# A feed forward in three token blocks in place of four, with seven-product multiplication in both of its weight matrices throughout

## The chip, the core and the metric

The kernel runs on one core of a Trainium2 chip, in one launch. The core has five engines that the text speaks of: PE (TensorE, the matrix multiplier), DVE (VectorE), ACT (ScalarE), POOL (GpSimd) and SP, whose queue issues every DMA of this kernel. The metric is device time in microseconds (us), the median of several runs. A difference of about 0.5% (12 us) is what a measurement of this kernel can tell from none.

## The reference, cut to what matters

One layer of a hybrid encoder: a mixer (a gated spatial MLP beside gated DeltaNet heads), then a feed forward. There are 2048 prompt tokens and 32 sample tokens, 2080 in all; the model is 1024 wide, the feed forward 4096. Everything is float32. The change touches the feed forward and the norm behind it alone:

```python
h = rmsnorm(x, norm_ffn_g[l]) * (1 + sc2) + sh2
x = x + gt2 * (jnp.square(jax.nn.relu(h @ w_up[l])) @ w_down[l])
...
y = rmsnorm(x, final_norm_g)
```

`h @ w_up` is (2080 x 1024) by (1024 x 4096), and `@ w_down` is (2080 x 4096) by (4096 x 1024).

## The kernel before

**How a float32 product is made.** A float32 value is split into a high part in PE's rounded type (`fp32r`) and the rest. `split` does it in two instructions: ACT copies the value into the high part, and DVE (or POOL) subtracts it from the value. A product then takes three matmuls (`mm3`): high weight by high value, high weight by low value, low weight by high value.

**Seven products instead of eight.** A 2 x 2 block product normally takes eight block products. The kernel uses a scheme of the Strassen-Winograd kind with seven, in which sums and differences of the quarters of both operands are multiplied. In the up multiplication the weights' sums S1 to S4 (`s1` to `s4` in `up_weights`) are made by POOL in block 0, split, and stored in DRAM (`su_d`); later blocks read them back. In the down multiplication, seven-product where `plain` is false, the weights' sums lie in `sd_d` as plain float32, and the values' differences T1 to T4 are made by POOL (`hidden`).

**Tiling.** The 2080 tokens are cut into `NB` = 4 blocks of two groups (g = 0, 1) of `G` = 260 tokens, so a matmul has 260 columns. The hidden width of 4096 is cut into 16 steps s of 256. An up step (`ffn_up`) has seven products of four k tiles, each an `mm3`: 84 matmuls. Two up steps (s = 2q, 2q + 1) make the hidden values of one q. A down q (`ffn_down`) has two steps u; each takes four quarters of the weights, makes seven products of four `mm3`, 84 matmuls, and adds the results to the accumulators `acc` in SBUF by DVE (`add`). Where `plain` holds, in block 0 and in q = 7 of every block, `ffn_down8` makes eight products, 96 matmuls a step.

**Order of the work.** In `feed_forward`, a block begins with two up steps; then down steps and up steps of the next q take turns. Around them: `h2_values(b)` normalises a block's input, builds its seven sums and stores them in DRAM (`th_d`), after up step 8 of the block before; `h2_load(b)` loads and splits them into `hp` (28 pieces in `BH` and `BL`), after up step 15 of the block before; `settle` adds the residual ahead of q = 6; `square` and `final` make the last norm and the output.

**Scheduling.** Every call records an instruction with its operands; `schedule` then lays out all of them by a list scheduler with a cost for each, due times taken from the matmuls, and a rule that a DVE and a POOL instruction with SBUF inputs alone take turns. The order on each engine's queue is fixed by that before the launch. Buffers are rings: `uw` (eight places of split up weights), `dw` (six of down weights), `uraw` and `draw` (raw weights), `rp8`, `rpa`, `rpb` (split hidden values), "fe" (six pieces for h2), "fk" (the first inner half's values, `keep`). A ring's place is written again only when its readers are done. PSUM's eight banks go round by `take` and `give`.

Of the kernel before, what the change touches and what calls it, by code (L numbers as in the profile page):

```python
# [31 lines left out]
G = 260  # L32
NB = T // (2 * G)
# [5 lines left out]
NSLOT = 25  # L39
# [283 lines left out]
class Kern:  # L323
# [211 lines left out]
    def setup(self):  # L535
# [103 lines left out]
        self.sd_d = [[dt(f"sd_d{u}_{i}", [P, 512]) for i in range(4)] for u in range(16)]  # L639
# [744 lines left out]
    def ffn_places(self):  # L1384
        rg = self.ring
        e = [(s, G * e) for s in (6, 7, 16, 22, 23) for e in range(4)]
        for tag, n in (("fe", 6), ("fs", 2), ("fx", 1), ("fp", 1), ("fu", 2), ("fv", 1), ("fr", 3), ("fk", 4)):
            rg(tag, e[:n], (P, G))
            e = e[n:]

    def fsegs(self, b, g):
        return [(0, G - NS, 0), (G - NS, NS, 1)] if (b, g) == (NB - 1, 1) else [(0, G, 0)]

    def h2_values(self, b):

        t0 = 2 * G * b
        r = [self.new("fs") for _ in range(2)]
        for g in range(2):
            self.dma(r[g], self.r2_d[:, t0 + G * g : t0 + G * g + G])
        for k in range(4):  # L1400
            h = []
            for kk in (k, k + 4):
                for g in range(2):
                    x = self.new("fe")
                    self.dma(x, self.x2_d[kk][:, t0 + G * g : t0 + G * g + G])
# [6 lines left out]
            put = lambda i, x: self.dma(self.th_d[b % 2][i][:, k], x)  # L1412
            put(0, b11)
            t1 = self.new("fe")
# [6 lines left out]
            t2 = self.new("fe")  # L1421
# [5 lines left out]
    def h2_load(self, b):  # L1427
        for i in range(7):
            for k in range(4):
                x = self.new("fe")  # L1430
                self.dma(x, self.th_d[b % 2][i][:, k])
                self.split(*self.hp[i][k], x, POOL if b and k % 2 else DVE)
# [11 lines left out]
    def operand(self, ring, x):  # L1444
        hi, lo = self.turn(ring)
        self.split(hi, lo, x)
        return hi, lo

    def up_weights(self, b, s):

        quad = lambda q: self.i["w_u"][s, q]
        if b == 0:
            a11, a12, a21, a22 = (self.raw(self.uraw, quad(q)) for q in range(4))
            s1, s2 = (self.turn(self.uraw) for _ in range(2))
            self.tt(s1, a21, a22, ALU.add, POOL)
            self.tt(s2, s1, a11, ALU.subtract, POOL)
        out = []

        def sum_(i, x):
            if b == 0:  # L1460
                hl = self.operand(self.uw, x)
                for e in range(2):
                    self.dma(self.su_d[s][i][e], hl[e].f32())
            else:
                hl = self.turn(self.uw)
                for e in range(2):
                    self.act(hl[e], self.raw(self.uraw, self.su_d[s][i][e]), AF.Copy)
            out.append(hl)

        plain = lambda q, x: out.append(self.operand(self.uw, x if b == 0 else self.raw(self.uraw, quad(q))))  # L1470
        if b:
            s1 = s2 = s3 = s4 = a11 = a12 = a22 = None
        plain(0, a11)
        sum_(1, s2)
        sum_(0, s1)
        if b == 0:
            s3 = self.turn(self.uraw) if len(self.uraw) > 6 else a11
            self.tt(s3, a11, a21, ALU.subtract, POOL)
        sum_(2, s3)
        if b == 0:  # L1480
            s4 = s2
            self.tt(s4, a12, s2, ALU.subtract, POOL)
        sum_(3, s4)
        plain(1, a12)
        plain(3, a22)
        return out

    def down_weights(self, b, u):

        quad = lambda q: self.i["w_d"][u, q]  # L1490
        if self.plain(b, u // 2):
            a = [self.raw(self.draw, quad(q)) for q in range(4)]
            out = [self.operand(self.dw, x) for x in a]
            if b == 0 and u % 2 == 0 and u < 14:
                a11, a12, a21, a22 = a
                for i, (o, x, y, op) in enumerate(((a22, a21, a22, ALU.add), (a21, a11, a21, ALU.subtract),
                                                   (a11, a22, a11, ALU.subtract), (a12, a12, a11, ALU.subtract))):
                    self.tt(o, x, y, op, POOL)
                    self.dma(self.sd_d[u][(0, 2, 1, 3)[i]], o)
            return out  # L1500
        return self.down_sums(b, u)

    def down_sums(self, b, u):
        quad = lambda q: self.i["w_d"][u, q]
        get = lambda x: self.raw(self.draw, x)
        sd = self.sd_d[u]
        if b == 1 and u % 2:
            a11, a12, a21, a22 = (get(quad(q)) for q in range(4))
            s1, s2 = (self.turn(self.draw) for _ in range(2))
            self.tt(s1, a21, a22, ALU.add, POOL)  # L1510
            self.dma(sd[0], s1)
            self.tt(a21, a11, a21, ALU.subtract, POOL)
            self.dma(sd[2], a21)
            self.tt(s2, s1, a11, ALU.subtract, POOL)
            self.dma(sd[1], s2)
            for x in (a11, a21, s2, a12, s1, a22):
                yield self.operand(self.dw, x)
# [216 lines left out]
    def ffn_down8(self, b, q, ops):  # L1734
# [23 lines left out]
        if b == NB - 1:  # L1758
            yield
# [105 lines left out]
```

## Time and profile before

| what | us |
|---|---|
| median of 3 runs (2377.20 to 2388.42) | 2378.14 |
| span of the profiled execution, first to last instruction | 2381.2 |
| start of the first feed-forward matmul, in the span | 1021.4 |
| start of the last one | 2369.3 |

Time up to 1021 us is the mixer and its output projection; from there to 2369 us runs the feed forward, and the last 12 us are the final norm of the last group and the store of it. The times below are microseconds from the span's start. In a window's row stand its length, then the busy time and the number of instructions of PE, PEld (weight loads, which run beside the matmuls), DVE, ACT and POOL, the granted clock of PE, the busy share of the DMA engines, and GB/s. In a timeline row stand the start in us, the length in us, the engine, the line of the kernel, the instruction, its output and inputs. In a group's row stand, behind the count, the busy time in us and the mean of one in ns, then the idle time ahead of it and what ended that. Most lines are those of helpers: L337 is `act`, L352 `tt`, L357 `stt`, L390 `dma`, L398 the matmuls.

### The profile page before, as it was taken

The page shows a single profiled execution, that of the slowest core. Times are in us where ns is not written, and L with a number is a line of the kernel's source. Part 1 is how long each engine was busy: PE and PEld are TensorE (multiplying, and loading weights), DVE is VectorE, ACT ScalarE, POOL GpSimd, SP SyncE. Part 2 cuts the span into 40 slices and gives each one's busy share as a digit, 9 for nine tenths or more (in the row PEclk, how much of TensorE's full clock was granted, in tenths as well). Part 3 has the DMA queues.
Part 4 walks back from the last instruction along what each step waited for, and adds up shares of the span by engine and source line. Part 5 has one row for each costly group of instructions (what it writes and reads, how often), then busy time and mean ns, then how long its engine had stood idle before and what let it go on. Part 6 is the DMA issues. An engine that isn't in the chain of part 4 may idle for free.

```text
span 2381.2 us, 53498 instructions
## 1 busy us (share of the span) xinstructions
PE 2336.3 (98%) x18834; PEld 2208.5 (93%) x18834; DVE 1727.3 (73%) x3981; ACT 1543.1 (65%) x3704; POOL 746.9 (31%) x1047
## 2 busy tenths in 40 slices
PE   7999999999999999999999999999999999999998
PEld 4977878999999888999999999999999999999998
DVE  6556657566665646598767778989788888778796
ACT  5465556555665435375555688787898777887774
POOL 2244321412433222445333353323531212511111
PEclk9999999999999999999999999999999999999999
DMA  9798667555467867887767788787888878776773
GB/s 322 227 320 283 198 192 247 151 175 184 150 193 231 255 198 238 270 284 262 267 215 243 248 261 273 265 277 252 272 280 276 271 257 276 251 261 219 245 234 107
DMA packets 393637, 573.29 MB, mean 241 GB/s; under 512 B 73916, under 2 KB 207696, under 8 KB 393368
## 3 DMA queue, kind: packets, MB, share of 16 engines
q1 hardware_dynamic: 393368, 569.88, 73.7%
q8 instruction: 148, 2.42, 0.4%
q14 instruction: 121, 0.99, 0.1%
HBM read 434.31 MB, written 135.40 MB: 239 GB/s over the span
## 4 chain that ended last, share of the span: by engine, by line
PE 38%; ACT 5%; DVE 3%; DMA 3%; POOL 2%; issue 1%; POOLq 0%; DVEq 0%; SPq 0%; ACTq 0%
PE f L398 38%; ACT s L337 3%; DVE s L352 2%; POOL s L352 1%; DMA s<-su_d 1%; ACT wh L337 1%; ACT BH L337 1%; DMA wr<-su_d 1%; DVE s L357 0%; ACT wl L337 0%; POOL BL L352 0%; DVE wl L352 0%; DMA s<-w_u 0%; DMA s<-th_d 0%; DMA wr<-w_d 0%
## 5 line engine op out<-in xcount | busy, mean ns | idle before, releaser
L337 ACT ACTIVATE s<-s 128x260 f32<-128x260 f32 (+9 forms) x1379 | 600.9, 463 | 342.4 <-DVE s L357 100.3
L398 PE MATMUL f<-s,s 128*128 128x260 f32 x4068 | 537.8, 283 | 1.1 <-ACT s L337 0.4
L352 POOL TENSOR_TENSOR s<-s,s 128x260 f32<-128x260 f32 (+3 forms) x354 | 354.7, 1014 | 513.4 <-ACT s L337 379.2
L398 PE MATMUL f<-BH,wh 128*128 128x260 f32 x1796 | 511.0, 285 | 4.2 <-DVE s L352 3.8
L398 PEld LDWEIGHTS f<-s,s 128*128 128x128 f32 x4068 | 507.6, 188 | 3.6 <-DVE s L352 1.7
L398 PE MATMUL f<-BH,wl 128*128 128x260 f32 x1796 | 508.4, 283 | 1.0 <-DVE wl L352 1.0
L398 PE MATMUL f<-BL,wh 128*128 128x260 f32 x1796 | 507.1, 282 | 0.0
L352 DVE TENSOR_TENSOR s<-s,s 128x512 fp32r<-128x512 f32 (+5 forms) x721 | 406.8, 579 | 64.9 <-ACT s L337 40.5
L352 DVE TENSOR_TENSOR s<-f,s 128x260 f32<-128x260 f32 x856 | 347.8, 420 | 125.5 <-PE f L398 117.6
L398 PE MATMUL g<-BH,wh 128*128 128x512 f32 (+2 forms) x1112 | 421.7, 379 | 2.2 <-ACT BH L337 2.2
L398 PE MATMUL g<-BH,wl 128*128 128x512 f32 (+2 forms) x1112 | 392.0, 352 | 0.0
L398 PE MATMUL g<-BL,wh 128*128 128x512 f32 (+2 forms) x1112 | 390.8, 351 | 0.6 <-DVE BL L352 0.6
L398 PEld LDWEIGHTS f<-BH,wh 128*128 128x128 f32 x1796 | 338.7, 189 | 6.4 <-DVE s L352 2.2
L398 PEld LDWEIGHTS f<-BH,wl 128*128 128x128 f32 x1796 | 339.0, 189 | 1.8 <-DVE wl L352 1.8
L398 PEld LDWEIGHTS f<-BL,wh 128*128 128x128 f32 x1796 | 339.2, 189 | 0.0
L352 POOL TENSOR_TENSOR s<-s 128x260 f32<-128x260 f32 (+11 forms) x315 | 159.3, 506 | 465.2 <-DVE s L352 170.1
L337 ACT ACTIVATE wh<-s 128x512 fp32r<-128x512 f32 (+1 forms) x369 | 229.0, 629 | 55.5 <-PE f L398 17.6
L398 PEld LDWEIGHTS g<-BH,wh 128*128 128x128 f32 x1112 | 210.7, 189 | 25.8 <-issue 6.1
L398 PEld LDWEIGHTS g<-BH,wl 128*128 128x128 f32 x1112 | 209.7, 189 | 19.3
L398 PEld LDWEIGHTS g<-BL,wh 128*128 128x128 f32 x1112 | 210.9, 190 | 15.8 <-DVE BL L352 1.0
L398 PE MATMUL f<-BH,s 128*128 128x260 f32 x1016 | 225.3, 283 | 0.0
L357 DVE SCALAR_TENSOR_TENSOR s<-s,s,s 128x128 f32<-128x128 f32 (+5 forms) x318 | 164.0, 531 | 72.0 <-ACT s L337 44.1
(119 smaller groups left out, 3518.4 us busy)
## 6 DMA issues: line engine op xcount, KB each, us to landing
s<-su_d SPq DMA_DIRECT2D x288, 256.0 KB, 4.1
s<-w_u SPq DMA_DIRECT2D x171, 256.0 KB, 3.9
s<-w_d SPq DMA_DIRECT2D x151, 256.0 KB, 4.3
s<-sd_d SPq DMA_DIRECT2D x106, 256.0 KB, 4.4
wr<-su_d SPq DMA_DIRECT2D x96, 256.0 KB, 3.9
wr<-w_b SPq DMA_DIRECT2D x42, 512.0 KB, 4.7
wr<-w_d SPq DMA_DIRECT2D x70, 256.0 KB, 4.6
s<-x_d SPq DMA_DIRECT2D x128, 130.0 KB, 3.8
```

Source lines behind the costliest of these rows:

```text
L337: self.p.op(ACT, c, lambda: nc.scalar.activation(out=R(out), in_=R(in_), func=func, **{k: R(v) for k, v in kw.items()}), [out, accum], [in ...
L352: self.p.op(eng, c, lambda: e.tensor_tensor(out=R(out), in0=R(a), in1=R(b), op=op), [out], [a, b])
L357: self.p.op(DVE, c, lambda: nc.vector.scalar_tensor_tensor(out=R(out), in0=R(a), scalar=R(s), in1=R(b), op0=op0, op1=op1), [out], [a, s, b])
L398: nc.tensor.matmul(R(out), R(l), R(r), **kw)
```

## The change

The tokens are cut into three blocks of 2 x 348, 2 x 348 and 2 x 344. `plain` holds for q = 7 of the last block alone, so block 0, and q = 7 of the first two blocks, use the seven-product down. All down weights' sums are made in block 0, each step's four, by POOL; all sums, of up and down, are kept in DRAM in split form (high and low part), and later blocks load the parts straight into their places, with no instruction of ACT or DVE. One ring of nine places (`wr`) holds all split weights, one of eight all raw ones (`raws`), one of 14 pairs (`rp`) all split hidden values. The first inner half's values (B11 and T1) are split at the head of the odd up step instead of in the even one. The differences of hidden values are made by DVE instead of POOL. `h2_load(1)` splits all its pieces with DVE. `hp` lies in thirds of BH and BL: columns 0 to 347, 348 to 695 and 696 to 1043 of each in turn, and the last four pieces elsewhere. Three more slots of SBUF are taken (28), and the scratch for DMA of other queues is made smaller. The two settings of the block size and the functions in core:

```diff
-G = 260
-NB = T // (2 * G)
+GB = [348, 348, 344]
+FT = [0, 696, 1392]
+G = 348
+NB = 3
...
-NSLOT = 25
+NSLOT = 28
...
     def h2_load(self, b):
+        w = slice(0, GB[b])
         for i in range(7):
             for k in range(4):
-                x = self.new("fe")
-                self.dma(x, self.th_d[b % 2][i][:, k])
-                self.split(*self.hp[i][k], x, POOL if b and k % 2 else DVE)
+                x = self.piece("fe", b)
+                self.dma(x, self.th_d[b % 2][i][:, k, w])
+                hi, lo = self.hp[i][k]
+                self.split(hi[:, w], lo[:, w], x, POOL if b > 1 and k % 2 else DVE)
...
-    def operand(self, ring, x):
+    def operand(self, ring, x, keep=None):
         hi, lo = self.turn(ring)
+        w = slice(0, x.shape[1])
+        hi, lo = hi[:, w], lo[:, w]
         self.split(hi, lo, x)
+        for d, v in zip(keep or (), (hi, lo)):
+            self.dma(d, v.f32())
         return hi, lo

+    def kept(self, ring, src):
+        hl = self.turn(ring)
+        for v, d in zip(hl, src):
+            self.dma(v.f32(), d)
+        return hl
+
     def up_weights(self, b, s):
...
+        get = lambda q: self.raw(self.raws, quad(q))
+        su, wr = self.su_d[s], self.wr
         if b:
...
+            return [self.operand(wr, get(0)), self.kept(wr, su[1]), self.kept(wr, su[0]), self.kept(wr, su[2]),
+                    self.kept(wr, su[3]), self.operand(wr, get(1)), self.operand(wr, get(3))]
+        a11, a21, a22, a12 = (get(q) for q in (0, 2, 3, 1))
+        s1, s2 = (self.turn(self.raws) for _ in range(2))
+        self.tt(s1, a21, a22, ALU.add, POOL)
+        self.tt(s2, s1, a11, ALU.subtract, POOL)
+        out = [self.operand(wr, a11), self.operand(wr, s2, su[1]), self.operand(wr, s1, su[0])]
+        self.tt(a21, a11, a21, ALU.subtract, POOL)
+        out.append(self.operand(wr, a21, su[2]))
+        self.tt(s2, a12, s2, ALU.subtract, POOL)
+        out.append(self.operand(wr, s2, su[3]))
+        return out + [self.operand(wr, a12), self.operand(wr, a22)]

     def down_weights(self, b, u):
...
+        if b:
+            for q, k in ((0, None), (None, 2), (None, 1), (1, None), (None, 0), (3, None), (None, 3)):
+                yield self.kept(wr, sd[k]) if q is None else self.operand(wr, get(q))
+            return
+        a11, a21, a22, a12 = (get(q) for q in (0, 2, 3, 1))
+        s1, s2 = (self.turn(self.raws) for _ in range(2))
+        self.tt(s1, a21, a22, ALU.add, POOL)
+        self.tt(a21, a11, a21, ALU.subtract, POOL)
+        self.tt(s2, s1, a11, ALU.subtract, POOL)
+        yield self.operand(wr, a11)
+        yield self.operand(wr, a21, sd[2])
...
     def plain(self, b, q):
-        return b == 0 or q == 7
+        return (b, q) == (NB - 1, 7)
...
+        third = lambda v: [v[:, G * e : G * e + G] for e in range(3)]
+        cut = lambda *ss: [x for s in ss for x in third(sl(s, 0, (P, SLOT)))]
+        more = cut(4, 6, 7)
+        places = [hl for k in range(KT) for hl in zip(third(self.BH[k]), third(self.BL[k]))]
+        places += list(zip(more[:4], more[4:8]))
+        self.hp = [places[4 * i : 4 * i + 4] for i in range(7)]
+        r = cut(*hid) + more[8:]
+        self.rp = list(zip(r[::2], r[1::2]))
...
-        if s == 0:
-            self.keep = [[self.new("fk") for _ in range(2)] for _ in range(2)]
-        W = self.take()
+        if s % 2 == 0:
+            self.keep = [[self.piece("fk", b) for _ in range(2)] for _ in range(2)]
+        else:
+            for m in range(2):
+                k0, k1 = self.keep[0][m], self.keep[1][m]
...
+                self.put(ops, "B11", m, k0)
+                self.tt(k0, k1, k0, ALU.subtract)
+                self.put(ops, "T1", m, k0)
+        W = take()
...
-        elif s % 2 and g == 1:
-            self.tt(k1, t, k1, ALU.subtract, POOL)
+        if g == 1:
+            self.tt(k1, t, k1, ALU.subtract)
             put("T3", k1)
-            self.tt(k0, t, k0, ALU.subtract, POOL)
+            self.tt(k0, t, k0, ALU.subtract)
             put("T2", k0)
             put("B22", t)
```

`piece(tag, b)` takes a ring's buffer in the block's width; `put` splits a value into the next pair of `rp`; `ffn_last`, for the last block's q = 7, is `ffn_down8` in the order that the last block had.

More of the change, by code (lines that the diff above doesn't have):

```diff
@@ L1411, in h2_values @@
             b11, b12, b21, b22 = h
-            put = lambda i, x: self.dma(self.th_d[b % 2][i][:, k], x)
+            put = lambda i, x: self.dma(self.th_d[b % 2][i][:, k, : GB[b]], x)
             put(0, b11)
-            t1 = self.new("fe")
+            t1 = self.piece("fe", b)
             self.tt(t1, b12, b11, ALU.subtract)
@@ L1451, in up_weights @@
         quad = lambda q: self.i["w_u"][s, q]
[L1452 to L1468, printed above, removed]
@@ L1501, in down_weights @@
[L1501 to L1517, printed above, removed]
-            self.tt(a12, a12, s2, ALU.subtract, POOL)
-            self.dma(sd[3], a12)
-            yield self.operand(self.dw, a12)
-        else:
-            for x in (quad(0), sd[2], sd[1], quad(1), sd[0], quad(3), sd[3]):
-                yield self.operand(self.dw, get(x))
+        get = lambda q: self.raw(self.raws, quad(q))
@@ L1576, in feed_forward, with take @@
                 then = {}
-                for u, _ in enumerate(self.ffn_down8(b, q, ops) if self.plain(b, q) else self.ffn_down(b, q, ops)):
-                    if q < 7 and u < 2:
+                for u, _ in enumerate(self.ffn_last(b, q, ops) if self.plain(b, q) else self.ffn_down(b, q, ops)):
+                    if q < 7:
                         up(b, 2 * q + 2 + u, then)
                 ops = then
-    def take(self):
+    def take(self, w):
         b = self.fbanks.pop(0)
         self.banks["f"] = [b]
-        return b, self.bank("f")[:, :G]
+        return b, self.bank("f")[:, :w]
     def give(self, *banks):
@@ L1593, in ffn_up @@
         e = s % 2
+        width = slice(0, GB[b])
+        take = lambda: self.take(GB[b])
         def product(n, i, ps, start):
@@ L1691, in add @@
                 self.stt(a[:, ss], ps[:, ss], self.modc[:, 5, m, c : c + 1], a[:, ss], ALU.mult, ALU.add)
+        if q == 7 and last:
+            self.square(b, m, g)
     def ffn_down(self, b, q, ops):
         w = [self.down_weights(b, 2 * q + u) for u in range(2)]
+        pair = lambda: [self.take(GB[b]) for _ in range(2)]
         def product(name, ps, start, wu):
@@ L1703, in product, with add @@
                         self.mm3(ps[j][1], wh[:, c], wl[:, c], *ops[name][k], start and k == 0, k == 1, skip_group_check=True)
-        def add(ps, ms, g, first=False):
+        def add(ps, ms, g, first=False, last=False):
             for j, m in enumerate(ms):
-                self.add(b, q, m, g, ps[j][1], first)
+                self.add(b, q, m, g, ps[j][1], first, last)
         for u in range(2):
@@ L1769, in square @@
             return
-        x = self.new("fp" if end and m == 7 else "fx")
+        x = self.piece("fp" if end and m == 7 else "fx", b)
         self.act(x, a, AF.Square)
```

194 lines of the change are left out of this document (84 added, 110 removed).

## The prediction

> **What bounds the kernel now.** I read the page first, then the window view with the last stage cut at its four token blocks, then the step of a matmul in the timeline.
>
> ```profile
> span 2381.2 us, 53498 instructions
> PE 2336.3 (98%) x18834; PEld 2208.5 (93%) x18834; DVE 1727.3 (73%) x3981; ACT 1543.1 (65%) x3704; POOL 746.9 (31%) x1047
> ...
> L337 ACT ACTIVATE s<-s 128x260 f32<-128x260 f32 (+9 forms) x1379 | 600.9, 463 | 342.4 <-DVE s L357 100.3
> L398 PE MATMUL f<-s,s 128*128 128x260 f32 x4068 | 537.8, 283 | 1.1 <-ACT s L337 0.4
> ```
> ```profile
> core 0: us, PE busy (x) PEld busy (x) DVE busy (x) ACT busy (x) POOL busy (x), PEclk, DMA share, GB/s
> 1021.40:1372.00 350.60, 347.49 (x2878) 345.11 (x2875) 271.56 (x493) 205.13 (x470) 149.20 (x119) 1.00 0.76 253
> 1372.00:1705.00 333.00, 330.53 (x2733) 328.12 (x2732) 291.83 (x597) 269.95 (x615) 127.04 (x128) 1.00 0.82 269
> 1705.00:2038.00 333.00, 331.32 (x2739) 330.00 (x2738) 279.43 (x606) 269.53 (x629) 88.36 (x105) 0.99 0.82 268
> 2038.00:2369.30 331.30, 330.41 (x2746) 329.71 (x2744) 264.56 (x596) 247.09 (x569) 66.90 (x83) 1.00 0.68 223
> sum 1347.90, PE 1339.75 PEld 1332.94 DVE 1107.38 ACT 991.71 POOL 431.49; mean PE 334.94 PEld 333.24 DVE 276.85 ACT 247.93 POOL 107.87
> ```
>
> The feed forward takes 1347.9 us of the span, and the matmul engine is busy in nearly all of it. Its matmuls follow from the loops: 84 per up step, 84 per seven-product down step, 96 per plain one. Block 0 (plain) has 16 x (84 + 96) = 2880, each later one, plain in its last q alone, 16 x 84 + 14 x 84 + 2 x 96 = 2712; together 11,016. The windows show these and a few of the norm. A busy engine may still be slow, so the step from start to start counts:
>
> ```profile
> 2085.00:2335.00 250.00, 250.00 (x2081) 250.00 (x2080) 1.00 0.74 242
> ```
> ```profile
> 1011.38 0.35 PE L398 MATMUL g<-BL,wh 128*128 128x400 f32 x1
> ...
> 1014.31 0.34 PE L398 MATMUL g<-BH,wl 128*128 128x400 f32 x1
> ```
> ```profile
> 875.25 0.39 PE L398 MATMUL g<-BL,wh 128*128 128x512 f32 x1
> ...
> 877.56 0.39 PE L398 MATMUL g<-BH,wl 128*128 128x512 f32 x1
> ```
>
> With 260 columns a step is 250.00/2081 = 120.1 ns; with 400, 16 steps in 2.93 us, 183 ns; with 512, 10 steps in 2.31 us, 231 ns. So a matmul costs about 0.444 ns a column and almost nothing per instruction. 11,016 x 120.1 = 1323 us; the other 25 us are holes, most at block starts. **The matmul stream is the bound**, and only fewer columns or fewer holes shorten it.
>
> **What the change does to the matmuls.** Three blocks: 2688 + 2688 matmuls of 348 columns, and 1344 + 14 x 84 + 192 = 2712 of 344; 8088 in all. Interpolated, 348 columns cost 159.7 ns through 400 and 158.8 through 512; I take 159.5, and 157.7 for 344. Sum: 857.5 + 427.7 = 1285 us, **38 us less**. Most of it is block 0, which had eight products.
>
> The Trainium skill (TensorE: Matmul & The Clock Gate, Back-to-back issue gap) gives an isolated gap of N/2.4 + 2.5 ns; by it the step would be 110.8 and 147.5 ns and the gain 32 us. The trace has 120.1 and 231 (215.8 by the rule), so it does not agree, and the rows are used.
>
> **What VectorE gets in block 0.** Here the change adds work: the down weights are now summed and split there in full, as the up weights are. VectorE and GpSimd prices:
>
> ```profile
> 1109.70 0.69 DVE L352 TENSOR_TENSOR wl<-s,wh 128x512 fp32r<-128x512 f32 x1 [0.36 <-issue]
> 1110.31 0.42 DVE L352 TENSOR_TENSOR s<-f,s 128x260 f32<-128x260 f32 x1
> 1110.65 0.42 DVE L352 TENSOR_TENSOR s<-s 128x260 f32<-128x260 f32 x1
> 1110.99 0.68 DVE L352 TENSOR_TENSOR wl<-s,wh 128x512 fp32r<-128x512 f32 x1
> 1111.59 0.42 DVE L352 TENSOR_TENSOR s<-s 128x260 f32<-128x260 f32 x1
> ```
> ```profile
> 1099.52 1.29 POOL L352 TENSOR_TENSOR s<-s 128x512 f32<-128x512 f32 x1 [11.43 <-DMA su_d<-wl]
> 1100.89 4.49 POOL L352 TENSOR_TENSOR s<-s,s 128x512 f32<-128x512 f32 x3
> ```
>
> From start to start VectorE needs 0.60 us for 512 columns and 0.34 for 260, so 0.43 for 348 (records overlap by 0.08); GpSimd needs 1.29 for 512. One up step with one down step is 168 x 159.5 = 26.8 us of matmuls, and asks of VectorE: 14 weight splits x 0.60 = 8.4; 7 splits and 4 differences of hidden values x 0.43 = 4.7 (the differences were GpSimd's); 5 + 14 adds out of PSUM x 0.43 = 8.2. That is 21.3 us, and 341 for 16 pairs. Beside it in block 0: `h2_values(1)` 24 x 0.43 = 10; `h2_load(1)`, now wholly VectorE's, 28 x 0.43 = 12; the half of `h2_load(0)` that comes late, 6; `settle` 16 x 0.49 = 8 and the scaled adds of q 6 and 7, +3; less 16 first adds that ScalarE copies, -7. Sum **373 us**, against 428.7 of matmuls. That alone would hide. But GpSimd has 128 sums x 1.29 = 165 us there, with h2's eight 173, and the two stop each other:
>
> ```profile
> 1102.06 2.72 DVE L352 TENSOR_TENSOR s<-wr,s 128x512 fp32r<-128x512 f32 x2
> ```
> ```profile
> L352 DVE TENSOR_TENSOR wl<-s,wh 128x512 fp32r<-128x512 f32 x114 | 97.5, 866 | 18.1 <-ACT wh L337 16.3 <-issue 0.4
> L352 DVE TENSOR_TENSOR s<-f,s 128x260 f32<-128x260 f32 x160 | 66.4, 423 | 37.7 <-PE f L398 37.1
> L352 DVE TENSOR_TENSOR s<-s,s 128x512 fp32r<-128x512 f32 x32 | 27.1, 868 | 3.7 <-ACT s L337 3.7
> L352 DVE TENSOR_TENSOR s<-s,s 128x260 fp32r<-128x260 f32 x48 | 22.1, 475 | 5.2 <-ACT s L337 4.9
> L352 DVE TENSOR_TENSOR s<-wr,s 128x512 fp32r<-128x512 f32 x26 | 19.7, 778 | 1.2 <-ACT s L337 1.0
> L352 DVE TENSOR_TENSOR BL<-s,BH 128x260 fp32r<-128x260 f32 x38 | 18.1, 493 | 1.1 <-ACT BH L337 0.9
> ```
>
> These are block 0's groups. Two splits under GpSimd's sums took 2.72 us instead of 1.3. Alone a split takes 0.68 (the 1110.99 row), so the three wide groups lost 114 x 0.18 + 32 x 0.18 + 26 x 0.09 = 29 us, the narrow ones with 0.42 alone 48 x 0.055 + 38 x 0.07 = 5; adds out of PSUM lost nothing (0.423). That is 34 of GpSimd's 149.2 us, 23% (a floor, as smaller groups are left out). In the densest stretch it is more:
>
> ```profile
> 1040.00:1080.00 40.00, 38.48 (x319) 38.09 (x319) 36.28 (x53) 29.18 (x67) 21.57 (x16) 1.00 0.86 284
> ```
> ```profile
> L352 DVE TENSOR_TENSOR wl<-s,wh 128x512 fp32r<-128x512 f32 x19 | 18.5, 1004 | 1.5 <-ACT wh L337 1.2
> L352 DVE TENSOR_TENSOR s<-s,s 128x260 fp32r<-128x260 f32 x8 | 5.5, 692 | 0.0
> L352 DVE TENSOR_TENSOR s<-s,s 128x512 fp32r<-128x512 f32 x4 | 4.2, 1094 | 0.0
> ```
>
> 19 x 0.32 + 8 x 0.27 + 4 x 0.41 = 9.9 of 21.57 us, 46%. I take a third of 173, 57 us, between the two. VectorE then needs 430 us, and it is never full:
>
> ```profile
> 1620.00:1680.00 60.00, 59.77 (x497) 59.42 (x496) 57.75 (x123) 47.28 (x104) 15.09 (x15) 1.00 0.87 291
> ```
>
> Here it is 96% busy and the matmuls still run. 430/0.96 = **448 us for block 0**, 19 over its matmuls: half of the gain is given back.
>
> **The other terms.** Blocks 1 and 2 lose work: the sums come back already split, by DMA, so 8 ScalarE copies of an up step and 4 splits of a down step go. VectorE has 6 x 0.60 + 12.9 = 16.5 of 26.8 us a pair, GpSimd almost nothing; the matmuls cover it all, and I leave 6 us of holes each (block 2 before has 333.0 - 325.7 = 7.3, block 3 5.6): 434.7 and 433.7. DMA in block 0: 24 x 0.262 MB x 16 + 19 MB of activations = 120 MB in 448 us, 267 GB/s, what block 1 before carries (269); so nothing. Nine weight places for both kinds instead of eight and six are eight products x 1.9 us = 15 us ahead, over the 4 us of a landing; nothing, and up to 5 us if the SP queue holds loads behind the 16 stores a pair that wait for splits.
>
> The splits of B11 and T1 move from the even up step to the odd one. They are wanted by the next down step, which begins one up step (13.4 us) later: nothing. The differences' chain is the tight one: T3 needs the add after the fifth product, relu, square, difference, split and rest, six instructions of some 0.45 us (the page's L337 group has 463 ns, VectorE 0.43), 2.7 us with no hand-over; the two products left and B11 cover 5.7. Two stops behind a sum of 1.29 us still fit; a third does not, and then the matmuls wait. What queues behind such a stopped difference on VectorE are the adds that free PSUM banks. The smaller scratch for DMA touches nothing: the page's issues are all SPq.
>
> At the start a hole is new. A third of the `h2_load(0)` pieces goes to columns 696 to 1043 of BH and BL, which the last matmuls of the output projection read, and they share two of the six "fe" buffers. Each takes a landing and a split, 4.5 us, after the one before; the fourth comes 12 us after the start and is wanted after four products, 7.7. Price 5 us; as VectorE is behind there anyway I take half, 2.5 (before, the start has few holes: 18.62 of 20 us busy).
>
> ```profile
> s<-th_d SPq DMA_DIRECT2D x112, 130.0 KB, 3.3
> ```
> ```profile
> 1021.00:1041.00 20.00, 18.62 (x143) 17.32 (x142) 1.00 0.87 281
> ```
>
> The end (2369.3 to 2381.2) has the same steps on 344 instead of 260 columns, +1 us. What lies before 1021 us is the same work.
>
> Sum: 448 + 434.7 + 433.7 = 1316.4, against 1347.9: -31.5; with +2.5 and +1, **-28 us**. 2381.2 - 28 = 2353; the median of the runs lies 3.1 under the span, so **2350 us**, 1.2% less.
>
> **Rivals.** (1) *Block 0 fits*: GpSimd's sums fall on VectorE's adds out of PSUM (130 us of them, of 173), which nothing stops. For it speaks the x160 row (0.423); against it that the adds come when a product ends. Block 0 is then 434: 2336, at the cheaper 348-column step 2330.
>
> (2) *The two engines' turns become the bound, and it is slower.* VectorE's instructions with both inputs in SBUF are 14 x 0.60 + 11 x 0.43 = 13.1 us a pair, GpSimd's 10.3, of 26.8. If VectorE stands still for 65% of GpSimd's time, block 0 is (373 + 112)/0.96 = 505 and the time 2407; for all of it, 569 and 2471. It is even where block 0 is 476, a share of 49%, and over 0.5% slower from 55%. The dense stretch, at 46%, is close to that, with few adds in it; the block's mean is far.
>
> The Trainium skill (SBUF - State Buffer, SBUF: two separate sides) calls this an exclusive lock held for the whole instruction, by which the loser stops fully; the 2.72 us row agrees. Taken alone, it says 2471.
>
> (3) *The block starts*: the full 5 us at the start, and 26.8 us of the last two down steps must hold `h2_load(1)` (12 us), 28 adds x 0.49 and 14 splits (8.4), 34 us on VectorE. A hole there also slows the clock:
>
> ```profile
> 1705.56 0.28 PE L398 MATMUL f<-BH,wl 128*128 128x260 f32 x1
> ...
> 1708.56 0.42 PE L398 MATMUL f<-BH,wh 128*128 128x260 f32 x1
> 1708.78 0.42 PE L398 MATMUL f<-BL,wh 128*128 128x260 f32 x1
> ```
>
> (0.22 a step after the hole.) Price 2.5 + 7 + 2 = 12: 2362.
>
> **Chances.** Forecast (2340 to 2358) 0.46, (1) 0.18, (3) 0.20 (2355 to 2378), (2) 0.16. 0.5% is 12 us, about what a measurement can tell. Under 2366: the forecast, (1) and two fifths of (3), 0.72; the rest of (3) and a quarter of (2) within, 0.16; above 2390, 0.12. Range 2330 (the floor of (1)) to 2380 (a blocked share of 46% with (3)'s holes).
>
> **What would show it.** Right: a 348-column step of 159 to 160 ns; block 0 near 450 us with VectorE over 93% busy, wide splits over 0.87 us on average, and matmuls waiting for VectorE; blocks 1 and 2 under 437 with VectorE under 75%. Wrong: block 0 under 437 (rival 1) or over 476 (2), holes of several us at 1021 or at the change of block (3), or a step that is not 159.5, at 8 us for each ns.

## The result and the profile after

| | before | after |
|---|---|---|
| median of 4 runs, us | 2379.35 | 2355.99 (2351.13 to 2358.92) |
| ratio to the kernel before, with its 95% interval | | 0.9891 [0.9867, 0.9916] |
| span of the profiled execution, us | 2381.2 | 2355.2 |
| first feed-forward matmul, us | 1021.4 | 1026.8 |
| feed forward, first to last start, us | 1347.9 | 1315.3 |

The change makes the kernel 23 us faster, 1.1%. The forecast was 2350 us, 28 us less, with a range of 2330 to 2380.

The page of the kernel after, against the same rows of before:

```profile
span 2355.2 us, 45713 instructions
...
PE 2304.7 (98%) x15888; PEld 2173.7 (92%) x15888; DVE 1667.3 (71%) x3675; ACT 1226.0 (52%) x2818; POOL 597.4 (25%) x827
...
L339 ACT ACTIVATE s<-s 128x348 fp32r<-128x348 f32 (+13 forms) x1079 | 494.8, 482 | 348.0 <-DVE s L354 136.3
L400 PE MATMUL f<-s,wh 128*128 128x348 f32 (+1 forms) x2760 | 661.4, 322 | 5.8 <-DVE s L359 2.4
```

Over the whole span every engine has less to do: 2946 matmuls fewer, ACT 317 us less, POOL 150 us less, DVE 60 us less. None of this says where the limit lies, as the whole span mixes the blocks. The windows do. This is the window view of the kernel after, cut at the first matmul of each of the three blocks, then two short stretches in which matmuls wait, and a long one in which they do not (columns as in the prediction):

```profile
core 0: us, PE busy (x) PEld busy (x) DVE busy (x) ACT busy (x) POOL busy (x), PEclk, DMA share, GB/s
1026.80:1474.10 447.30, 438.21 (x2696) 432.40 (x2695) 434.82 (x747) 269.95 (x546) 208.79 (x143) 0.99 0.77 261
1474.10:1911.30 437.20, 435.14 (x2708) 434.00 (x2707) 323.73 (x646) 216.70 (x463) 46.78 (x45) 0.99 0.81 266
1911.30:2342.20 430.90, 430.90 (x2741) 430.37 (x2740) 291.59 (x604) 191.46 (x401) 29.71 (x29) 1.00 0.65 214
1026.80:1046.80 20.00, 18.10 (x101) 16.89 (x100) 19.64 (x31) 14.87 (x33) 9.26 (x7) 0.91 0.99 329
1440.00:1495.00 55.00, 51.00 (x294) 48.77 (x294) 48.59 (x91) 32.77 (x71) 32.15 (x25) 0.94 0.76 254
1080.00:1380.00 300.00, 299.96 (x1875) 298.64 (x1874) 290.75 (x496) 180.27 (x356) 144.47 (x98) 1.00 0.76 262
```

Block 0 takes 447 us, and VectorE (DVE) is busy for 434.8 of them, 97%. In block 1 it is 74% busy, in block 2 68%. The same view for the matmul line alone, in a stretch of block 0 and one of block 2 (PE, PEld, clock, DMA share, GB/s):

```profile
1080.00:1380.00 300.00, 299.96 (x1875) 298.64 (x1874) 1.00 0.76 262
1960.00:2320.00 360.00, 360.00 (x2284) 360.00 (x2284) 1.00 0.65 211
```

360.00/2284 is 157.6 ns a matmul of 344 columns. 300.00/1875 is 160.0 for 348; from start to start, with the few slower steps left aside, it is 159.53. In these 300 us of block 0 the matmuls stand still for 0.04 us, while VectorE is busy for 290.75. So although VectorE is full there, the matmuls do not wait for it all along. They wait in three places: at the start, around 1390 us, and around 1446 to 1467 us. What they wait for in block 0 (total us, times, longest):

```profile
PE f L400 <- DVE s L354: 2.7, 3, 1.2
PE f L400 <- DVE s L359: 2.4, 1, 2.4
PE f L400 <- ACT s L339: 1.7, 3, 0.7
PE f L400 <- DVE BL L354: 1.3, 1, 1.3
PE f L400 <- ACT BH L339: 0.6, 1, 0.6
PE f L400 <- DVE wl L354: 0.3, 1, 0.3
```

Most of this is VectorE: splits and differences of hidden values (s, L354), `settle` (L359), pieces of h2 (BL). These waits are 9.0 us. Called a hole below is every step, from one feed-forward matmul to the next, that is over a quarter too long, with what it exceeds the step by: 18.5 us in block 0, 8.2 in block 1 and 3.4 in block 2. Beside the waits this holds matmuls at a slower clock behind them (0.91 and 0.94 granted in the two short rows) and the few matmuls of the norm that lie between (1.7, 2.7 and 2.7 us).

What VectorE does in block 0, from the group view with shapes kept apart (count, then busy us and mean ns of one):

```profile
L354 DVE TENSOR_TENSOR wl<-s,wh 128x512 fp32r<-128x512 f32 x145 | 116.6, 818 | 4.8 <-ACT wh L339 4.5
L354 DVE TENSOR_TENSOR s<-f,s 128x348 f32<-128x348 f32 x232 | 112.6, 506 | 4.8 <-PE f L400 4.2
L354 DVE TENSOR_TENSOR s<-s,s 128x348 fp32r<-128x348 f32 x116 | 70.1, 624 | 1.0 <-ACT s L339 1.0
L354 DVE TENSOR_TENSOR s<-s,s 128x348 f32<-128x348 f32 x70 | 49.3, 713 | 0.6 <-ACT s L339 0.6
L354 DVE TENSOR_TENSOR wl<-wr,wh 128x512 fp32r<-128x512 f32 x55 | 44.8, 820 | 0.0
```

An instruction of 512 columns alone has a record of 0.68 us, one of 348 columns 0.51 (the prediction's steps with the 0.08 us by which records overlap). So the four groups with both inputs in SBUF lose 145 x 0.138 + 116 x 0.114 + 70 x 0.203 + 55 x 0.14 = 55 us to GpSimd. Over all groups, instruction by instruction, the loss is 68 us, 33% of GpSimd's 208.8. The x232 row, the adds out of PSUM, loses nothing (506 against 510). The same count gives 361 us of work without the loss. **361 + 68 = 430 us**, as the prediction had it.

### The profile page after: what moved, and what is told of

The parts are those of the page before. It is cut to its first block, busy times and chain, and to the rows that moved or that the text cites. A ratio compares the mean times of both kernels' runs of the same rounds, so it can differ in the third digit from the quotient of the medians.

```text
span 2355.2 us, 45713 instructions
## 1 busy us (share of the span) xinstructions
PE 2304.7 (98%) x15888; PEld 2173.7 (92%) x15888; DVE 1667.3 (71%) x3675; ACT 1226.0 (52%) x2818; POOL 597.4 (25%) x827
## 4 chain that ended last, share of the span: by engine, by line
PE 83%; DMA 6%; DVE 6%; ACT 3%; issue 2%; POOL 1%; SPq 0%; POOLq 0%; DVEq 0%; ACTq 0%
PE f L400 50%; PE g L400 24%; PE C L400 3%; DVE s L354 2%; ACT s L339 2%; PE B L400 2%; PE L L400 1%; DVE s L359 1%; DMA pk_d<-s 1%; DVE wl L354 1%; DMA s<-ada 1%; PE M L400 1%; PE L L411 1%; DVE BL L354 1%; DMA s<-xT 1%
## 5 line engine op out<-in xcount | busy, mean ns | idle before, releaser
L339 ACT ACTIVATE s<-s 128x348 fp32r<-128x348 f32 (+13 forms) x1079 | 494.8, 482 | 348.0 <-DVE s L354 136.3
L400 PE MATMUL f<-s,wh 128*128 128x348 f32 (+1 forms) x2760 | 661.4, 322 | 5.8 <-DVE s L359 2.4
L400 PEld LDWEIGHTS f<-s,wh 128*128 128x128 f32 x2760 | 479.4, 188 | 9.2 <-DVE s L354 3.5
L354 DVE TENSOR_TENSOR s<-f,s 128x348 f32<-128x348 f32 (+1 forms) x696 | 347.6, 511 | 179.3 <-PE f L400 178.3
L400 PE MATMUL f<-s,wl 128*128 128x348 f32 (+1 forms) x1380 | 443.6, 321 | 0.3 <-DVE wl L354 0.3
L354 DVE TENSOR_TENSOR s<-s,s 128x348 fp32r<-128x348 f32 (+7 forms) x688 | 356.0, 545 | 58.1 <-ACT s L339 24.1
L400 PE MATMUL f<-BL,wh 128*128 128x348 f32 (+1 forms) x1016 | 328.9, 324 | 2.2 <-DVE BL L354 2.2
L400 PE MATMUL f<-BH,wh 128*128 128x348 f32 (+1 forms) x1016 | 328.3, 323 | 1.7 <-ACT BH L339 1.7
L400 PE MATMUL f<-BH,wl 128*128 128x348 f32 (+1 forms) x1016 | 328.5, 323 | 0.0
L354 POOL TENSOR_TENSOR s<-s,s 128x512 f32<-128x512 f32 (+5 forms) x154 | 188.7, 1233 | 304.0 <-ACT s L339 148.2
L354 POOL TENSOR_TENSOR s<-s 64x39 f32<-64x39 f32 (+12 forms) x299 | 156.7, 524 | 426.7 <-issue 381.0
L400 PEld LDWEIGHTS f<-s,wl 128*128 128x128 f32 x1380 | 259.8, 188 | 0.7 <-DVE wl L354 0.6
L354 DVE TENSOR_TENSOR wl<-s,wh 128x512 fp32r<-128x512 f32 (+1 forms) x278 | 211.2, 768 | 19.2 <-ACT wh L339 18.9
L359 DVE SCALAR_TENSOR_TENSOR s<-s,s,s 128x128 f32<-128x128 f32 (+5 forms) x318 | 163.5, 529 | 71.9 <-ACT s L339 43.8
L354 DVE TENSOR_TENSOR wl<-wr,wh 128x512 fp32r<-128x512 f32 (+2 forms) x161 | 153.5, 956 | 63.9 <-ACT wh L339 61.1
```

The costliest lines, as they stand in the source:

```text
L339: self.p.op(ACT, c, lambda: nc.scalar.activation(out=R(out), in_=R(in_), func=func, **{k: R(v) for k, v in kw.items()}), [out, accum], [in ...
L354: self.p.op(eng, c, lambda: e.tensor_tensor(out=R(out), in0=R(a), in1=R(b), op=op), [out], [a, b])
L359: self.p.op(DVE, c, lambda: nc.vector.scalar_tensor_tensor(out=R(out), in0=R(a), scalar=R(s), in1=R(b), op0=op0, op1=op1), [out], [a, s, b])
L400: nc.tensor.matmul(R(out), R(l), R(r), **kw)
```

## The experiments

Diffs are against the kernel after. Below, "block 0" is the time from its first matmul to the first of block 1, "work" is VectorE's instructions at their lengths alone, and "standing" is what their records exceed these by behind GpSimd, both counted as above. The theory is the prediction's: block 0 exceeds its 429 us of matmuls because VectorE's work and its standing behind GpSimd fill it. The rivals are a hole at the start that is a cost of its own, VectorE's work alone whatever GpSimd does, and the time that a sum takes ahead of what waits for it, whether VectorE is full or not.

**The same kernel again** (one execution), for the spread between two executions.

> The changed kernel once more, to see what is the kernel's and what is one execution's. Blocks 447, 437 and 431 us again within 2 us each if these are the program's. The first feed-forward matmul came 5.4 us later than before (1026.8 against 1021.4), though the first 7150 PE records have the same order; if 3.5 us of that is the execution, this run starts at 1021 to 1025, and if it is the program, at 1026 to 1027.

```profile
1023.20:1471.20 448.00, 438.78 (x2697) 432.40 (x2696) 434.46 (x747) 270.26 (x546) 209.74 (x143) 0.99 0.77 261
```

2355.78 us; blocks of 448.0, 437.0 and 432.8 (447.4, 437.2 and 430.8 in the first execution), with holes in the same places. Block 2, whose code no run below but the one of the differences changes, took 430.5 to 433.5 us in the others, so a block's length in one execution is read to about 3 us. The feed forward began 3.5 us earlier. The kernel before, run again beside the experiments, took 2380.1 to 2381.0 us (three medians of seven).

**Without the sums** (one execution). The weights' sums and differences of block 0 are left out, and plain quarters stand in for them.

```diff
-        self.tt(s1, a21, a22, ALU.add, POOL)
-        self.tt(s2, s1, a11, ALU.subtract, POOL)
-        out = [self.operand(wr, a11), self.operand(wr, s2, su[1]), self.operand(wr, s1, su[0])]
-        self.tt(a21, a11, a21, ALU.subtract, POOL)
+        out = [self.operand(wr, a11), self.operand(wr, a21, su[1]), self.operand(wr, a22, su[0])]
...
```

> Left out: all sums of weights in block 0 (128 on GpSimd); quarters stand in for them, and are split, stored and multiplied as before. Theory A (VectorE stands behind GpSimd's sums for 65 us and is full for that reason): wide splits under 0.72 us on average, VectorE busy 375 us or less of block 0, block 0 436 us (433 to 439), only the holes at its start left. Theory B (the holes come from the start, the residual and h2 work crowding, and the SP queue, whatever GpSimd does): block 0 443 us or more.

The window view of block 0 and of its first 20 us, then the group of wide splits:

```profile
1023.90:1454.20 430.30, 430.17 (x2700) 429.75 (x2699) 384.81 (x761) 273.64 (x559) 20.12 (x20) 1.00 0.82 277
...
1023.90:1043.90 20.00, 19.87 (x129) 19.55 (x128) 18.72 (x38) 17.12 (x39) 2.54 (x3) 1.00 0.97 319
```
```profile
L354 DVE TENSOR_TENSOR wl<-s,wh 128x512 fp32r<-128x512 f32 x151 | 101.6, 685 | 2.5 <-ACT wh L339 2.0
```

2332.54 us. Block 0 is 430.3, 17 less, which is its matmuls and 1.5 us: nearly the whole surplus went, and VectorE fell to 89% busy (384.8 us; 375 or less was expected). The split is back at 685 ns, where it is without GpSimd, and the standing at 5.9 us. More went than expected, as the holes at the start went as well (19.87 of 20 us busy, against 18.10). Those had been put down to landings and two shared buffers; neither was touched here. The run takes away the standing and the wait for a sum together, so it does not tell these two apart.

**The sums on VectorE** (one execution): the eight `tt` that make the sums lose their `, POOL`. This removes the standing and adds 128 x 0.60 = 77 us of work.

```diff
-        self.tt(s1, a21, a22, ALU.add, POOL)
+        self.tt(s1, a21, a22, ALU.add)
...
```

> Block 0's 128 sums made by VectorE. Theory A, with VectorE's work as the price: 65 us of standing still mostly go, 128 x 0.60 = 77 us of work come, block 0 about 465 us (458 to 472), wide splits under 0.72 us. Theory C (what costs is the time of GpSimd's sums ahead of the splits, 1.3 us against 0.6, not VectorE's time): block 0 447 us or less.

```profile
1026.40:1471.90 445.50, 436.53 (x2697) 430.53 (x2695) 442.10 (x869) 265.97 (x545) 20.52 (x18) 1.00 0.76 261
```

2358.55 us, block 0 445.5 us. The 465 of theory A was too much: the standing is 5.3 us and the work 434.8, so the sum of both is 440, against 430 in the kernel after, and yet block 0 is no longer than there. VectorE is busy for 442.1 of 445.5 us, 99%: the prediction's 0.96 was no ceiling, and with that number the theory gave too long a time. The 445.5 us lie where theory C had them (447 or less), but they speak little for it. A sum takes 0.57 us here instead of some 1.5, and the holes of block 0 fall only from 18.5 to 16.7, while those of block 1 grow from 8.2 to 12.0; blocks 0 and 1 together take 886.4 us, and 884.6 in the kernel after. Nor do that kernel's matmuls wait for what a sum precedes, the split weights: 0.3 us of 9.0, in the rows above. That a late sum delays other work through the queues is not excluded by this; the run with half of h2 on GpSimd, below, shows a case.

What a sum on GpSimd costs VectorE in standing, some 0.5 us on average (63 us for 128 sums), is about what VectorE needs to make it itself, 0.57 (73.5 us). Where they are made is a draw; that they are made is what costs. The Trainium skill (SBUF — State Buffer, SBUF: two separate sides) has one of the two engines hold a shared pair of ports for a whole instruction, against a VectorE instruction with two SBUF inputs; the x232 row, which has one input in PSUM and loses nothing, agrees. Why the loss is a third of GpSimd's time and not all of it was not tried. The sums get longer as well (1.52 us on average for the 125 of 512 columns in block 0 of the kernel after, against 1.29), so GpSimd stands for a part of it.

**The thirds in another order** (four runs). The first pieces of h2, which the first matmuls need, go to the columns of BH and BL that are free first.

```diff
-        places = [hl for k in range(KT) for hl in zip(third(self.BH[k]), third(self.BL[k]))]
+        places = [(third(self.BH[k])[e], third(self.BL[k])[e]) for e in range(3) for k in range(KT)]
```

> The h2 pieces go to the first third of all eight BH and BL, then the second, then the last, so that the columns which the output projection reads to its end are wanted by the fifth and sixth products. If the holes of the first 15 us come from these columns and from two of six buffers serving them (theory A): holes there fall from 5 us to under 2, block 0 to 443, the time by 3 to 4 us. If VectorE's backlog alone makes block 0 long (rival): the start is tighter, but as much is lost later, block 0 stays at 446 to 448 and the time is the same.

The window view of its block 0, of its first 20 us, and of the 300 us in which the kernel after has no hole:

```profile
1026.30:1474.70 448.40, 437.95 (x2696) 431.83 (x2695) 435.26 (x743) 268.96 (x541) 211.03 (x143) 0.99 0.76 259
1026.30:1046.30 20.00, 19.48 (x123) 18.89 (x122) 19.83 (x30) 14.99 (x34) 11.26 (x8) 1.00 0.99 321
...
1080.00:1380.00 300.00, 298.80 (x1860) 296.56 (x1859) 292.78 (x496) 179.12 (x353) 141.23 (x96) 1.00 0.75 259
```

2356.79 us, ratio 0.9897 [0.9872, 0.9921], the same as the kernel after. The time lost in the first 20 us, slower matmuls included, fell from 5.2 us to 1.7, and block 0 still took 448.4. The 3.5 us come back in pieces (by the starts of the matmuls in both traces): 1.3 more between 1047 and 1070 us, holes of 0.6 each at 1118, 1168 and 1225, where the kernel after has none, and 0.5 more around 1391. The waits among them are for VectorE. So the order of the pieces decides whether the holes lie at the start, but not what block 0 costs: VectorE is as far behind as before, and the matmuls meet its backlog later. And as the same holes went without the sums, landings untouched, the landings alone do not make them.

**The differences back on GpSimd** (one execution), as in the kernel before.

```diff
-                self.tt(k0, k1, k0, ALU.subtract)
+                self.tt(k0, k1, k0, ALU.subtract, POOL)
...
```

> Undoes one part: the differences of hidden values go back to GpSimd. In block 0 VectorE loses 64 x 0.43 = 27 us of work, GpSimd gets 64 x 0.94 = 60 us. Theory A (VectorE's time, work and standing together, sets block 0, and it stands for a third of GpSimd's time): net 27 - 20 = 7 us, block 0 about 441 us (437 to 446), standing 85 us or more; blocks 1 and 2 within 2 us. Theory D (VectorE's work alone counts, and the standing in block 0 is only time it would have idled): block 0 432 to 435.

The window view, the group of differences, and PE's waits between 1080 and 1380 us (total us, times, longest):

```profile
1023.50:1479.50 456.00, 440.18 (x2697) 431.47 (x2696) 440.31 (x682) 272.33 (x546) 280.85 (x207) 0.99 0.75 256
```
```profile
L354 POOL TENSOR_TENSOR s<-s,s 128x348 f32<-128x348 f32 x62 | 73.9, 1208 | 34.6 <-DVE s L354 16.1 <-ACT s L339 7.3 <-DMA s<-x_d 5.0
```
```profile
PE f L400 <- DVE s L354: 8.3, 9, 1.6
```

2364.47 us and block 0 456.0, more than either theory gave. The sum of work and standing is unchanged: 333.5 + 99.8 = 433. What is new is nine waits in the stretch in which the kernel after has none. One of them, in the timeline (start, length, then the operation, and in brackets what it waited for):

```profile
1228.01 0.42 PE L400 MATMUL f<-s,wh 128*128 128x348 f32 x1 [1.63 <-DVE s L354]
```
```profile
1221.44 4.63 POOL L354 TENSOR_TENSOR s<-s,s 128x348 f32<-128x348 f32 x4 [0.48 <-ACT s L339]
```
```profile
1224.50 3.45 DVE L354 TENSOR_TENSOR s<-s,s 128x348 fp32r<-128x348 f32 x3 [0.40 <-ACT s L339]
```

Four differences in a row hold GpSimd for 4.63 us, and the three splits behind them take VectorE 3.45 us instead of 1.3; the product that wants them is 1.6 us late. This is the chain of T3 that the prediction called the tight one. With the differences on VectorE it holds; by this run that part of the change is worth 8.6 us in block 0, at equal load.

**Half of h2 back on GpSimd** (one execution).

```diff
-                self.split(hi[:, w], lo[:, w], x, POOL if b > 1 and k % 2 else DVE)
+                self.split(hi[:, w], lo[:, w], x, POOL if b and k % 2 else DVE)
```

> Undoes one part: half of the second block's h2 pieces are split by GpSimd. Between 1440 and 1495 us the changed kernel has holes of 7.9 us. If VectorE's time is what is short there: 14 x 0.43 = 6 us of work go and 14 x 0.94 = 13 us of GpSimd's time come with some 4 us of standing, the holes stay at 6 to 9 us. If the pieces themselves are late because one engine makes all of them (the third rival of the prediction): holes of 4 us or less.

The window view of block 0 and of the change of block, as shown for the kernel after (447.30 and 51.00 of 55.00):

```profile
1026.60:1484.60 458.00, 442.06 (x2698) 434.49 (x2697) 440.82 (x746) 273.76 (x556) 223.53 (x157) 0.99 0.76 260
1440.00:1495.00 55.00, 46.59 (x269) 43.76 (x268) 46.32 (x80) 31.36 (x69) 36.85 (x31) 0.97 0.74 243
```

2363.65 us, worse than either theory had it. Block 0 became 10.6 us longer and block 1 4.2 shorter, as part of the hole moved ahead of the change of block. GpSimd has 15 us more, and matmuls stand still for 8.4 us of the 55 instead of 4. The longest hole, at 1464 us, can be followed back in the timeline (GpSimd, ScalarE, VectorE, PE):

```profile
1449.15 5.51 POOL L354 TENSOR_TENSOR BL<-s,BH 128x348 fp32r<-128x348 f32 x3 [4.00 <-ACT BH L339]
1454.62 1.73 POOL L354 TENSOR_TENSOR wr<-wr,s 128x512 f32<-128x512 f32 x1
...
1456.38 0.63 ACT L339 ACTIVATE wh<-wr 128x512 fp32r<-128x512 f32 x1 [2.37 <-POOL wr L354]
...
1458.87 1.23 DVE L354 TENSOR_TENSOR s<-s,s 128x348 fp32r<-128x348 f32 x2 [2.68 <-ACT s L339]
...
1464.04 3.45 PE L400 MATMUL f<-s,s 128*128 128x348 f32 x11 [2.93 <-DVE s L354]
```

Three of the pieces hold GpSimd for 5.5 us, and a weights' sum comes behind them in its queue. ScalarE stands for 2.37 us until that sum is there, and copies of hidden values come behind it; for these VectorE stands for 2.68 us, then works without a pause, and a matmul of block 0 waits 2.93 us for one of its splits. So what is late here is not a piece of h2 but what stands behind the pieces in three queues: VectorE, with fewer splits to make, was idle. The other holes were not followed back.

**Room for VectorE at q = 5** (four runs). The eight-product down, which needs no sums and four splits where the seven-product one needs seven, is used in block 0 at q = 5; the sums of that q are then made in block 1. It costs 24 matmuls more.

```diff
+LATE = (5,)
...
-        return (b, q) == (NB - 1, 7)
+        return (b, q) == (NB - 1, 7) or (b == 0 and q in LATE)
...
-        if b:
+        if b and not (b == 1 and u // 2 in LATE):
...
-        for g, u in ((0, 0), (0, 1), (1, 0), (1, 1)):
+        for g, u in ((0, 0), (0, 1), (1, 0), (1, 1)) if b else ((0, 0), (1, 0), (0, 1), (1, 1)):
...
-            if u == 1:
+            if b == 0 and g == 1:
+                yield
+            if b and u == 1:
...
```

> q = 5 of block 0 has eight products, with no sums; its weights' sums are made, split and stored in block 1, where VectorE has 110 us free. 24 matmuls more, 3.8 us; VectorE in block 0 gets 6 splits x 0.60, 8 differences and 6 splits of hidden values x 0.43, 12 adds x 0.43 and 8 sums' standing x 0.5 less, some 19 us. Theory A: block 0 437 us (434 to 440), block 1 436 to 439, the time 9 us less (2347). If block 0's holes do not come from VectorE's time: block 0 447 + 4 = 451 and 2360.

```profile
1024.90:1467.00 442.10, 438.10 (x2721) 434.49 (x2720) 420.16 (x716) 263.25 (x533) 195.42 (x135) 1.00 0.75 256
1467.00:1902.10 435.10, 432.57 (x2707) 430.73 (x2707) 330.54 (x653) 221.77 (x472) 56.02 (x53) 1.00 0.81 268
```

2349.51 us (2347.98 to 2350.39), ratio 0.9866 [0.9852, 0.9881]: 6.5 us better than the kernel after, and its four times all lie under the five of that kernel (2351.13 at the least). Block 0 came out at 442.1 us and not at the 437 of the theory, but with 24 x 159.5 ns = 3.8 us more of matmuls it is still 5.3 us shorter than the kernel after's; work and standing fell to 346.9 + 67.5 = 414. The holes at 1390 and at 1446 to 1467 us are gone, and those at the start, some 5 us, are left: about what is missing to the 437. The standing is as before (68 and 67.5), so it is VectorE's own work that fell; with it one q's chain of sums and differences went, and the two are not told apart. Block 1, which now makes the four sums of each of two steps, did not get longer.

**Combinations and other places** (four runs each). The same with the thirds in the other order; the same at q = 3 and 5; and at q = 1, each with the other order. Only `LATE` and the line of `places` differ.

> The same for q = 3 and q = 5, and the h2 pieces by thirds. 48 matmuls more, 7.7 us; VectorE some 38 us less in block 0, so it is no longer full and the gain at the start of the thirds' order should show. Theory A: block 0 428.7 + 7.7 + 2 = 438 us (437 to 441), with holes under 3 us in it; the time 8 to 10 us less. If one plain q already suffices, this is no better than that one; if VectorE was still short with one, it is 2 us or more better.

> q = 5 of block 0 plain, with the thirds' order of the h2 pieces. With one plain q block 0 still has 5.6 us of holes in its first 15 us and 1.8 us around 1060. If the start was VectorE's backlog alone, the thirds' order changes nothing again: block 0 442, 2349. If the order of the columns is worth something once the block has room later: holes of the first 20 us under 2, block 0 439, 2346.

> q = 1 plain instead of q = 5, the same order. Same work in all, but the room on VectorE comes early. If only the sum of VectorE's time in the block counts: block 0 within 2 us of the run with q = 5. If it counts where the room lies: fewer holes before 1070 us, but the ones where settle and h2's sums crowd (4 to 6 us, near 1390) come back; block 0 442 to 445.

| kernel | us | ratio | block 0 | VectorE busy in it |
|---|---|---|---|---|
| q = 5, thirds | 2348.07 | 0.9862 [0.9840, 0.9885] | 441.2 | 94% |
| q = 3 and 5, thirds | 2348.75 | 0.9870 [0.9854, 0.9887] | 443.7 | 89% |
| q = 1, thirds | 2349.87 | 0.9874 [0.9848, 0.9900] | 445.4 | 91% |

```profile
1028.80:1474.30 445.50, 440.31 (x2722) 435.37 (x2721) 404.92 (x710) 263.51 (x529) 199.55 (x135) 1.00 0.74 250
```

All three beat the kernel before. Against the kernel after, the first is clearly faster (all four times are under its least); the times of the other two, 2348.12 to 2353.67 and 2345.26 to 2356.32 us, overlap with it. Between the three and the q = 5 kernel above no difference can be measured. With q = 3 and 5 the fewest holes are left, 6.5 us (under 3 were expected), but 48 more matmuls cost 7.7, and block 0 came out 6 us over the forecast. With q = 5 the thirds' order takes the holes of the first 20 us from 4.8 to 1.6, as it was to, but block 0 from 442.1 to 441.2 alone and not to 439. The row is that of q = 1: VectorE is 10 us less busy than with q = 5 and the same order (414.5 us), yet block 0 is 4 us longer, with a hole of 1.7 us left at 1454.6. That the place of the room counts is not shown by it. Of the signs of that theory, the holes near 1390 did not come back (0.9 us), though 4.5 us lie between 1420 and 1460, where the run with q = 5 and the same order has none; those of the first 43 us are not fewer (5.3 against 4.5). The profile is of the slowest of its four runs, and the whole feed forward takes 1313.0 us in it, against 1312.6.

## Why the prediction was right, and where its steps were off

**The step** of a 348-column matmul is 159.53 ns (159.5 forecast) and of 344 columns 157.63 (157.7). Counted alike, the holes of the feed forward are 26.8 us in the kernel before and 30.2 after, so its matmuls went from 1347.9 - 26.8 = 1321 to 1315.3 - 30.2 = 1285 us: 36 less where the prediction had 38, as the old ones were 2 us cheaper than its 1323. Of these 36 us, 3.4 went back into holes. The prediction's "half of the gain is given back" sets block 0 against its matmuls alone; it is true of block 0, but the kernel before has holes of its own, as the prediction's sum allows, and those of its four blocks are gone. The Trainium skill (TensorE: Matmul & The Clock Gate, Back-to-back issue gap), by whose formula for an isolated matmul 348 columns would take an estimated 147.5 ns, is again not what the trace has.

**Block 0** is 447.4 us against 448, and here the parts came out, not only the sum: standing 68 where 57 was taken, work 361 where 373 was. The share of GpSimd's time was a third, as chosen between 23% and 46%; GpSimd's own time was 209 us, not 173: its sums get longer too (1.52 us on average, for 1.29; 1.42 and 1.45 in the rows below), and the rest of its work takes 19 us, for 8. Of the work, 12 us were not in the block: by the places of its instructions, part of `h2_load(1)` slips past the end of the block and more of `h2_load(0)` comes ahead of its start. The two misses cancel. The experiment without the sums shows that the sums make the surplus. But that 430/0.96 gave 448 is luck, as its constant is none: by it the kernel with the sums on VectorE would need 440/0.96 = 458 us for block 0, and takes 445.5, 99% busy; the one with q = 5 would need 431, and takes 442.1. The surplus is rather holes at three places where deferred work (`h2_values`, `settle`, `h2_load`) falls due. This is the one at 1390 us, in the timeline of the kernel after, for PE, DVE and POOL:

```profile
1389.98 0.42 PE L400 MATMUL f<-s,wh 128*128 128x348 f32 x1 [0.55 <-ACT s L339]
...
1391.56 0.43 PE L400 MATMUL f<-s,wh 128*128 128x348 f32 x1 [1.16 <-DVE s L354]
...
1394.99 0.95 PE L400 MATMUL f<-s,wh 128*128 128x348 f32 x2 [2.37 <-DVE s L359]
```
```profile
1389.49 3.54 DVE L354 TENSOR_TENSOR s<-s,s 128x348 fp32r<-128x348 f32 x3
...
1392.95 1.06 DVE L359 SCALAR_TENSOR_TENSOR s<-s,modc,s 128x348 f32<-128x348 f32 x2
```
```profile
1389.70 1.42 POOL L354 TENSOR_TENSOR wr<-s,s 128x512 f32<-128x512 f32 x1 [10.02 <-DVE wl L354]
1391.20 1.45 POOL L354 TENSOR_TENSOR s<-s 128x512 f32<-128x512 f32 x1
```

Three splits take 3.54 us instead of 1.3, beside two sums of GpSimd; `settle` (L359) comes after them in the queue, and the product whose bank it frees waits 2.37 us. The holes at the other two places were not followed in this way. The wide splits were to take over 0.87 us on average and took 0.82: the standing fell more on the 348-column instructions (the x70 row, 713 ns). That sign of the forecast did not come.

**Blocks 1 and 2**: 437.2 and 430.8 against 434.7 and 433.7, the same in sum; block 1 is not under 437, as a sign had it. VectorE is under 75% in both, as forecast. The holes are 8.2 and 3.4 us, where 6 each were left (2.7 of each are the norm's matmuls); all but 0.1 of block 1's lie in its first 20 us, at the change of block.

**The start, 2.5 us**, failed as a term. It was to come on top of block 0. The hole is there, and larger (5.2 us), but it lies inside the 448, and the experiment on the thirds shows that taking most of it away shortens nothing. **The end** is +1.3 us against +1 (11.9 us from the last start to the end before, 13.2 after).

**"What lies before 1021 us is the same work"** failed too: the feed forward begins 5.4 us later. The first 7000 matmul records are the same instructions in the same order; from record 7000 on, the window view of before, and then of after:

```profile
898.70:1021.40 122.70, 118.20 (x731) 114.62 (x730) 69.59 (x154) 55.05 (x121) 45.62 (x45) 0.97 0.82 257
```
```profile
902.20:1026.80 124.60, 119.48 (x731) 115.22 (x729) 66.79 (x143) 50.96 (x110) 43.38 (x42) 0.97 0.78 244
```

3.5 us of the shift are there already at record 7000, and the second execution of the same kernel does not have them (898.5): they belong to the execution. In the profiles of the experiments, which begin with the same 7000 matmuls, that record lies anywhere between 898.5 and 904.2. The other 1.9 us come behind it, and the second execution has them too (124.7 in place of 124.6). The stretch makes `h2_values` and `h2_load` of block 0 with wider pieces, but in the experiments, which have these too, it takes 121.3 to 125.8 us, so the width alone does not set it; what does was not tried.

**The sum.** In the spans: blocks 447.4 + 437.2 + 430.8 = 1315.4 for a forecast 1318.9 (the start among them), 3.5 better; the stretch ahead 5.4 worse; the end 0.3 worse. So the span is 2355.2 against 2353.2. The rest of the 6 us of the miss is the frame: the median was to lie 3.1 us under the span and lies 0.8 over it. The profiled execution of after took 2357.03 us, 1.8 over its span; with as much around its span, that of before took some 2383, over 3 us above the median of its kernel. A size was taken off that belongs to one execution.

**The rivals.** (1), that block 0 fits, holds only without the sums (430.3). (2), that the engines' turns become the bound, did not occur: the share is 33%, of more GpSimd time than was taken. By the prediction's rule the change is worth nothing where work and standing reach 476 x 0.96 = 457 us; the kernel after has 430, and the one with the differences on GpSimd 433. (3), holes at the start and at the change of block, named as a sign of a wrong forecast, are there: 5.2 us at the start, for 5, and 11.2 between 1440 and 1495 us. The rival was right in its places and near in its prices, and wrong in adding them to block 0.

## What to carry to other kernels

When matrix products are saved by making sums of operands, price the sums on the engine that splits and adds, with what it loses while another engine works beside it; here the sums cost 17 us of block 0, and it made no measurable difference on which of the two engines they were made. The full engine did not delay the bound all along here but at the few places where deferred work falls due, and a hole repaired at one of them came back at later ones. Taking load away helped: one q of the eight-product kind, 3.8 us of matmuls dearer, was worth 6.5 us net. A chain that passes between two engines that slow each other costs more than its load says: the same sum of work and standing took 8.6 us longer with the differences on GpSimd, and half of h2's splits there made block 0 10.6 us longer, with VectorE idle behind a late sum.

## What the hardware showed that was not expected

- The same instructions in the same order came 3.5 us later in one execution than in others (matmul record 7000 at 898.7 in the kernel before, 902.2 and 898.5 in two executions of the kernel after, 898.5 to 904.2 in all twelve profiles), so a forecast from one profiled execution has 3 us and more of its own.
- VectorE ran at 99% (442.1 of 445.5 us) with the matmuls hardly later than at 97% (blocks 0 and 1 in 886.4 us, against 884.6).
- Three splits next to two sums on GpSimd took 3.54 us instead of 1.3, while the adds out of PSUM, in the same block, took 506 ns, where without the sums they took 515.
